# A two-layer decoder trunk: three plain gate/up pairs a layer instead of four, low parts of two operand preparations by ScalarE and an adding DMA, norm weights loaded by ScalarE's queue

## The chip, the cores and the metric

The kernel runs on one core of a Trainium2 chip. The metric is the device time of one execution in microseconds (us), the median of three runs. Engines are named as the profile names them: PE is TensorE's matmul, PEld its weight load, DVE is VectorE, ACT is ScalarE, POOL is GpSimd, SP is SyncE; SPq, POOLq and ACTq are the queues on which these engines issue transfers.

## What is computed

A decoder trunk of two layers works on 512 tokens of width 1024, in float32: a mixer (attention in layer 0, causal pooling in layer 1), then a gated feed-forward block (FFN), each on a normalized input and added back. The change lies in the FFN of both layers and in the first loads.

```
def swiglu_ffn(h, w_gate_up, w_down):
    gu = h @ w_gate_up
    gate, up = gu[..., :D_FF], gu[..., D_FF:]
    return (jax.nn.silu(gate) * up) @ w_down

for i in range(DEPTH):                      # DEPTH = 2, D_MODEL = 1024, SEQ = 512, D_FF = 2816
    x = x + mixer(rmsnorm(x, mixer_norm))   # attention, then pooling
    x = x + swiglu_ffn(rmsnorm(x, ffn_norm[i]), w_ffn_gate_up[i], w_ffn_down[i])
return rmsnorm(x, final_norm)
```

## The kernel before, in words

**Numbers.** Every float32 operand is split into a high part (a rounded copy, type fp32r) and a low part (what is left). A product is three matmuls: high by high, high by low, low by high. `split` (L90) makes the two parts: ACT copies the value into the high part (L91), DVE subtracts the high part from the value and writes the low part (L92). `split_neg` (L94 to L96) does the same for the negated value.

**FFN.** The 2816 hidden columns are 22 blocks of 128. For each block j there is one gate and one up product, together a pair. The first `NPLAIN` = 4 pairs of a layer are plain (`plain_pair`, L1047): two products of 8 steps over the 1024 input columns, so 2 x 8 x 3 = 48 matmuls of 128x512. The other 18 use a Strassen-like scheme with seven half-size products (`strassen_pair` L1128, which calls `chained` L515 and `mult` L453): 7 x 4 x 3 = 84 matmuls of 128x256. The scheme needs sums and differences of quarters of the normalized input, `T["11", k]`, `T["1", k]` and so on, k = 0 to 3. `chained` starts with the product called "11" (into the PSUM tile alpha), then "1" (into gamma), "2" (added onto alpha), "21", "3", "22" and last "4"; ACT copies alpha and gamma away in between (L531, L535, L539, L547).

**Preparing T.** `prepare(k)` (L1062) makes the operands of one k while the plain pairs run. It takes two temporary buffers, `Temp()`, h and t (called temp in the rows); there are two such buffers in all, so each prepare writes those of the one before it. `normed` (L570) fills h with two scaled quarters of X (L574, two instructions) and t with the differences (L578, L579, L581). Then three splits of 128x512 (one of h, two of t) and one `split_neg` of 128x256 write the high and low parts into the room called far. In the kernel before, `plain_pair(j)` calls `prepare(j)` between its gate and its up product.

**Order after the plain pairs.** The blocks run in four parts, `PARTS` (L43). Part 0 holds blocks 0 and 1: after the plain pairs, its down product follows (8 outputs x 2 steps x 3 = 48 matmuls of 128x512, each output added to X by DVE, L1173), and then the Strassen pairs. Engine orders come from a scheduler: each engine has one queue and waits on semaphores in it.

**Weights.** A plain weight tile is loaded by SP, copied to its high part by ACT (L145), negated into its low part by ACT (L146), and the weights themselves are added to that by a transfer on POOL's queue with `accum_op` add (L148); this is called lean. A Strassen pair (`class Pair`, L153) loads its blocks by SP (L169 to L171), makes the sums b by an adding transfer on POOL's queue (L172), and ACT and DVE split four tiles of them (L91, L92), with two additions on DVE (L188, L189). Raw weights go through a ring of four buffers, split weights through a ring of five; a load waits until the ring's oldest buffer has been read.

**Start.** POOL's queue loads the norm weights nrm (L891), four dummy matmuls (`WARM`) run on PE, and for each k SP loads X[k] and the weights `w_first[k]`, for k = 0 in two halves that ACT copies one by one (L914, L915). DVE scales X[0] by nrm (L387).

## Time and profile before

| what | value |
|---|---|
| median of three runs | 1189.78 us (1189.6 to 1190.49) |
| profiled execution, own time | 1190.54 us |
| its span (first to last instruction) | 1188.8 us |
| PE busy | 1179.8 us, 99% of the span |
| DVE busy | 966.0 us, 81% |
| ACT busy | 711.9 us, 60% |
| POOL busy | 171.6 us, 14% |
| mean granted TensorE clock | 0.998 of full |
| transfers on the adding queue (software_dynamic) | 61.38 MB, 31.2% of 16 engines' span |

Rows of the timeline give a start in us from the span's start, a duration in us, the engine, the line, and the operation with its tiles; several like instructions in a row are one row (x2), and square brackets tell how long the engine had been idle and what ended that. Durations of neighbours overlap a little, so what an engine spends on one instruction is read from start to start. DMA rows give the size and the median us from issue to landing.

### The profile page before, as it was taken

The page shows a single profiled execution, that of the slowest core. Times are in us where ns is not written, and L with a number is a line of the kernel's source. Part 1 is how long each engine was busy: PE and PEld are TensorE (multiplying, and loading weights), DVE is VectorE, ACT ScalarE, POOL GpSimd, SP SyncE. Part 2 cuts the span into 40 slices and gives each one's busy share as a digit, 9 for nine tenths or more (in the row PEclk, how much of TensorE's full clock was granted, in tenths as well). Part 3 has the DMA queues.
Part 4 walks back from the last instruction along what each step waited for, and adds up shares of the span by engine and source line. Part 5 has one row for each costly group of instructions (what it writes and reads, how often), then busy time and mean ns, then how long its engine had stood idle before and what let it go on. Part 6 is the DMA issues. An engine that isn't in the chain of part 4 may idle for free.

```text
span 1188.8 us, 24883 instructions
## 1 busy us (share of the span) xinstructions
PE 1179.8 (99%) x9932; PEld 1118.4 (94%) x9932; DVE 966.0 (81%) x1693; ACT 711.9 (60%) x1244; POOL 171.6 (14%) x171
## 2 busy tenths in 40 slices
PE   9999999999999999999999999999999999999997
PEld 7889999999999988889999999988888999999997
DVE  6978798889788855699988997656879998898875
ACT  6545564456455546647756775685675775676553
POOL 1111111111111002311111111122130111111100
PEclk9999999999999999999999999999999999999999
DMA  8446666665766548857777777798695777777732
GB/s 276 130 98 158 157 156 154 172 160 147 202 144 158 152 145 207 190 117 187 197 194 190 191 191 191 207 266 207 128 194 108 193 194 196 200 194 190 197 93 72
DMA packets 82036, 205.19 MB, mean 173 GB/s; under 512 B 7648, under 2 KB 13184, under 8 KB 81920
## 3 DMA queue, kind: packets, MB, share of 16 engines
q1 hardware_dynamic: 51232, 141.96, 36.2%
q0 software_dynamic: 30544, 61.38, 31.2%
q8 instruction: 78, 1.28, 0.4%
q14 instruction: 38, 0.31, 0.1%
q10 hardware_dynamic: 144, 0.26, 0.1%
HBM read 201.48 MB, written 2.10 MB: 171 GB/s over the span
## 4 chain that ended last, share of the span: by engine, by line
PE 97%; issue 1%; ACT 1%; DMA 1%; DVE 0%; SPq 0%; POOL 0%; DVEq 0%; POOLq 0%; ACTq 0%
PE ps L457 20%; PE ps L459 19%; PE ps L458 19%; PE ps L325 9%; PE ps L326 8%; PE ps L328 8%; PE ps L628 2%; PE ps L630 2%; PE ps L629 2%; PE ps L921 2%; PE ps L840 1%; PE ps L712 1%; PE ps L732 1%; PE ps L834 1%; DMA x<-xT 1%
## 5 line engine op out<-in xcount | busy, mean ns | idle before, releaser
L91 ACT ACTIVATE w<-raw 128x1024 fp32r<-128x1024 f32 x265 | 280.5, 1063 | 171.3 <-PE ps L459 69.4
L92 DVE TENSOR_TENSOR w<-raw,w 128x1024 fp32r<-128x1024 f32 x265 | 323.0, 1222 | 52.2 <-ACT w L91 47.9
L457 PE MATMUL ps<-far,w 128*128 128x256 f32 x896 | 247.1, 276 | 0.3 <-ACT first L531 0.3
L459 PE MATMUL ps<-far,w 128*128 128x256 f32 x896 | 247.0, 276 | 0.0
L458 PE MATMUL ps<-far,w 128*128 128x256 f32 x896 | 247.0, 276 | 0.0
L457 PE MATMUL ps<-near,w 128*128 128x256 f32 x640 | 180.7, 282 | 0.0
L458 PE MATMUL ps<-near,w 128*128 128x256 f32 x640 | 177.4, 277 | 0.0
L459 PE MATMUL ps<-near,w 128*128 128x256 f32 x640 | 177.4, 277 | 0.0
L457 PEld LDWEIGHTS ps<-far,w 128*128 128x128 f32 x896 | 168.3, 188 | 0.5 <-ACT first L531 0.5
L458 PEld LDWEIGHTS ps<-far,w 128*128 128x128 f32 x896 | 168.3, 188 | 0.1
L459 PEld LDWEIGHTS ps<-far,w 128*128 128x128 f32 x896 | 168.3, 188 | 0.0
L325 PE MATMUL ps<-near,w 128*128 128x512 f32 (+1 forms) x332 | 125.8, 380 | 0.0
L328 PE MATMUL ps<-near,w 128*128 128x512 f32 (+1 forms) x332 | 125.2, 377 | 0.0
L326 PE MATMUL ps<-near,w 128*128 128x512 f32 (+1 forms) x332 | 125.1, 377 | 0.0
L457 PEld LDWEIGHTS ps<-near,w 128*128 128x128 f32 x640 | 120.6, 188 | 0.4
L458 PEld LDWEIGHTS ps<-near,w 128*128 128x128 f32 x640 | 120.4, 188 | 0.0
L459 PEld LDWEIGHTS ps<-near,w 128*128 128x128 f32 x640 | 120.4, 188 | 0.0
L172 POOL DMA_DIRECT2D raw<-w_pair x36 | 43.5, 1209 | 292.9 <-DMA raw<-w_pair 84.7
L328 PEld LDWEIGHTS ps<-near,w 128*128 128x128 f32 x332 | 62.4, 188 | 11.5
L325 PEld LDWEIGHTS ps<-near,w 128*128 128x128 f32 x332 | 62.3, 188 | 11.5 <-ACT near L91 0.4
L326 PEld LDWEIGHTS ps<-near,w 128*128 128x128 f32 x332 | 62.5, 188 | 11.2 <-DVE near L92 0.2
L91 ACT ACTIVATE half<-rawhalf 128x512 fp32r<-128x512 f32 x81 | 51.0, 631 | 14.6 <-PE ps L459 12.5
(311 smaller groups left out, 2763.3 us busy)
## 6 DMA issues: line engine op xcount, KB each, us to landing
raw<-w_pair SPq DMA_DIRECT2D x80, 512.0 KB, 4.8
raw<-w_qkp SPq DMA_DIRECT2D x36, 512.0 KB, 4.2
raw<-w_pair POOLq DMA_DIRECT2D x36, 512.0 KB, 7.6
raw<-w_dblock SPq DMA_DIRECT2D x32, 512.0 KB, 4.8
raw<-w_v SPq DMA_DIRECT2D x18, 512.0 KB, 4.4
raw<-w_qkp POOLq DMA_DIRECT2D x18, 512.0 KB, 7.6
rawhalf<-w_pair SPq DMA_DIRECT2D x36, 256.0 KB, 5.2
raw<-w_dblock POOLq DMA_DIRECT2D x16, 512.0 KB, 7.6
```

Of the source, the lines that this page charges most:

```text
L91: nc.scalar.activation(hi, v, AF.Copy)
L92: nc.vector.tensor_tensor(lo, v, hi.bitcast(F32), op=OP.subtract)
L172: nc.gpsimd.dma_start(self.b.rearrange("p (a c) -> p a c", a=2), self.src[:, None, 3 * n:].to_broadcast([P, 2, n]), accum_op=OP.add)
L325: nc.tensor.matmul(self.p[:, cols], w[0][:, s], mh[:, cols], start=self.done == 0, stop=False)
L326: nc.tensor.matmul(self.p[:, cols], w[0][:, s], ml[:, cols], start=False, stop=False)
L328: nc.tensor.matmul(self.p[:, cols], w[1][:, s], mh[:, cols], start=False, stop=self.done == self.n)
L457: nc.tensor.matmul(dst, w.t[0][:, c], th, start=k == 0 and not on, stop=False, skip_group_check=on)
L458: nc.tensor.matmul(dst, w.t[0][:, c], tl, start=False, stop=False, skip_group_check=on)
L459: nc.tensor.matmul(dst, w.t[1][:, c], th, start=False, stop=k == n - 1, skip_group_check=on)
L628: nc.tensor.matmul(o, mh, wh, start=k == 0, stop=False)
L629: nc.tensor.matmul(o, mh, wl, start=False, stop=False)
L630: nc.tensor.matmul(o, ml, wh, start=False, stop=k == K2 - 1)
```

## The change

`NPLAIN` falls from 4 to 3, so that pair 3 of each layer becomes a Strassen pair; it then runs after the down product of part 0 instead of before it. The four prepares stand in three pairs: prepare(0) in pair 0, prepare(1) in pair 1, prepare(2) at the end of pair 1, prepare(3) in pair 2. In prepare(1) and prepare(2) the three 128x512 splits are made by `moved`: ACT writes the high part, ACT writes its negative into the low part, and a transfer on POOL's queue adds the value from the temporary buffer. Norm weights are loaded on ACT's queue, `w_first[0]` comes in one transfer with one ACT copy, and there are five dummy matmuls.

```
-NPLAIN = 4
-WARM = 4
+NPLAIN = 3
+WARM = 5
...
+    def moved(hi, lo, v):
+
+        nc.scalar.activation(hi, v, AF.Copy)
+        nc.scalar.activation(lo, hi.bitcast(F32), AF.Copy, scale=-1.0)
+        nc.gpsimd.dma_start(lo, v.bitcast(F32R), accum_op=OP.add)
...
-            nc.gpsimd.dma_start(nrm, norms)
+            nc.scalar.dma_start(nrm, norms)
...
                 nc.sync.dma_start(X[k], xT[:, k, :])
+                nc.sync.dma_start(raw[:, s], w_first[k])
                 if k:
-                    nc.sync.dma_start(raw[:, s], w_first[k])
                     scaled(0, k, *U[k])
                     nc.scalar.activation(hi[:, s], raw[:, s], AF.Copy)
                 else:
-                    for e in range(2):
-                        c = slice(e * NF * P // 2, (e + 1) * NF * P // 2)
-                        nc.sync.dma_start(raw[:, c], w_first[k][:, c])
-                        nc.scalar.activation(hi[:, c], raw[:, c], AF.Copy)
+                    nc.scalar.activation(hi[:, s], raw[:, s], AF.Copy)
                     scaled(0, k, *U[k], on_dve=True)
...
-                prepare(j)
+                prepare((0, 1, 3)[j])
...
                 nc.vector.tensor_mul(up, up, gt)
+                if j == 1:
+                    prepare(2)
...
+                parted = moved if k in (1, 2) else split
                 h, t = normed(op, k, row, Temp(), Temp(), True)
...
-                split(b[:, 0].rearrange("p (a c) -> p a c", a=2), b[:, 1].rearrange("p (a c) -> p a c", a=2), hq[:, :, 0])
+                parted(b[:, 0].rearrange("p (a c) -> p a c", a=2), b[:, 1].rearrange("p (a c) -> p a c", a=2), hq[:, :, 0])
...
-                    split(b[:, 0], b[:, 1], t.t[:, i * S:(i + 1) * S])
+                    parted(b[:, 0], b[:, 1], t.t[:, i * S:(i + 1) * S])
```

Lines of the changed kernel are six higher than before in the body (L574 becomes L580, L92 stays), and some late ones differ by three or six. The engine orders move at these places of layer 0's FFN; layer 1 has the same tiles with small exchanges.

**DVE around prepare(2).** Before, the rows from its first instruction (temp_6099 is its h, temp_6100 its t; names in square brackets are the semaphores waited for, DMASW ones belong to POOL's transfers, DMAHW ones to SP's):

```order
L574 SCALAR_TENSOR_TENSOR temp_6099<-x_5169,nrm_75,row_5959 128x512
L574 SCALAR_TENSOR_TENSOR temp_6099<-x_5173,nrm_75,row_5959 128x512
L578 TENSOR_TENSOR temp_6100<-temp_6099 128x2x256 [waits DVE_49]
L92 TENSOR_TENSOR far_5857<-temp_6099,far_5857 128x512 [waits Activation_49]
L579 TENSOR_TENSOR temp_6100<-temp_6100,temp_6099 128x256 [waits DVE_49]
L96 SCALAR_TENSOR_TENSOR far_5857<-temp_6099,far_5857 128x256 [waits Activation_49]
L581 SCALAR_TENSOR_TENSOR temp_6100<-temp_6100,temp_6099 128x256 [waits DVE_49]
L1056 TENSOR_TENSOR u_6060<-ps_6114,row_5959 128x512 [waits PE_49]
L92 TENSOR_TENSOR far_5857<-temp_6100,far_5857 128x512 [waits Activation_49]
```

The same place of the changed kernel, up to the first instruction of prepare(3) (temp_6060 and temp_6061 are prepare(2)'s, temp_6108 is prepare(3)'s h; w_6155 and raw_5906 belong to the weights of pair 3):

```order
L580 SCALAR_TENSOR_TENSOR temp_6060<-x_5168,nrm_75,row_5960 128x512 [waits DMASW3_49,DVE_49]
L580 SCALAR_TENSOR_TENSOR temp_6060<-x_5172,nrm_75,row_5960 128x512
L92 TENSOR_TENSOR near_82<-up_6008,near_82 128x512 [waits Activation_49]
L194 TENSOR_TENSOR raw_5906<-raw_5906,raw_5907 128x512 [waits DMAHW2_49,DMAHW3_49,DMAHW1_49,DMAHW4_49,DMAHW0_49,DMASW5_49]
L92 TENSOR_TENSOR w_6155<-raw_5907,w_6155 128x1024 [waits DMASW4_49,Activation_49]
L584 TENSOR_TENSOR temp_6061<-temp_6060 128x2x256 [waits DMASW5_49,DMASW4_49,DVE_49]
L102 SCALAR_TENSOR_TENSOR far_5853<-temp_6060,far_5853 128x256 [waits Activation_49]
L585 TENSOR_TENSOR temp_6061<-temp_6061,temp_6060 128x256 [waits DVE_49]
L1059 TENSOR_TENSOR u_6080<-ps_6123,row_5960 128x512 [waits PE_49]
L587 SCALAR_TENSOR_TENSOR temp_6061<-temp_6061,temp_6060 128x256 [waits DVE_49]
L1061 TENSOR_TENSOR u_6080<-u_6080,gt_6106 128x512 [waits DVE_49]
L580 SCALAR_TENSOR_TENSOR temp_6108<-x_5169,nrm_75,row_5960 128x512 [waits DMASW6_49,DVE_49]
```

The three subtractions L92 into far are gone, and the first writes to h and t wait for a transfer of POOL (DMASW), which the rows before did not.

**DVE in prepare(3).** Before, its t and the low parts made from it:

```order
L578 TENSOR_TENSOR temp_6174<-temp_6173 128x2x256 [waits DVE_49]
L92 TENSOR_TENSOR far_5857<-temp_6173,far_5857 128x512 [waits Activation_49]
L579 TENSOR_TENSOR temp_6174<-temp_6174,temp_6173 128x256 [waits DVE_49]
L96 SCALAR_TENSOR_TENSOR far_5857<-temp_6173,far_5857 128x256 [waits Activation_49]
L581 SCALAR_TENSOR_TENSOR temp_6174<-temp_6174,temp_6173 128x256 [waits DVE_49]
L92 TENSOR_TENSOR w_6224<-raw_5979,w_6224 128x1024 [waits DMASW0_49,Activation_49]
```

In the changed kernel (x_5168 and others are the sums of the down product, w_6200 belongs to pair 4; the last row makes the low part of T["1", 3] and T["2", 3]):

```order
L1179 TENSOR_TENSOR x_5167<-x_5167,ps_6163 128x512 [waits PE_49]
L584 TENSOR_TENSOR temp_6109<-temp_6108 128x2x256 [waits DMASW7_49,DMASW1_49]
L1179 TENSOR_TENSOR x_5168<-x_5168,ps_6185 128x512 [waits PE_49]
L585 TENSOR_TENSOR temp_6109<-temp_6109,temp_6108 128x256 [waits DVE_49]
L92 TENSOR_TENSOR w_6200<-raw_5978,w_6200 128x1024 [waits DMAHW7_49,DMASW0_49,Activation_49]
L587 SCALAR_TENSOR_TENSOR temp_6109<-temp_6109,temp_6108 128x256 [waits DVE_49]
L92 TENSOR_TENSOR far_5853<-temp_6109,far_5853 128x512 [waits Activation_49]
```

prepare(3) now stands among the additions of the down product, and its t waits for two transfers.

**POOL's queue.** Before, from the low parts of the plain weights to the second Strassen pair that still lacks its sums (a transfer waits for the semaphore that it counts up itself, so DMASW3 in a row is also that row's own):

```order
L148 DMA w_5915<-w_pair 128x1024 [waits DMASW0_49,PE_49,Activation_49]
L172 DMA raw_5979<-w_pair 128x2x512 [waits DMAHW3_49,DMAHW4_49,DMAHW2_49,DMAHW5_49,DMAHW1_49,DMAHW7_49,DMAHW0_49,DMASW1_49]
L148 DMA w_5973<-w_pair 128x512 [waits DMASW2_49,PE_49,Activation_49]
L148 DMA w_5973<-w_pair 128x512 [waits DMASW3_49]
L148 DMA w_6051<-w_down 128x4x256 [waits DMASW4_49,PE_49,Activation_49]
L172 DMA raw_6091<-w_pair 128x2x512 [waits DMAHW5_49,DMAHW3_49,DMAHW6_49,DMAHW1_49,DMASW5_49]
L148 DMA w_6086<-w_down 128x4x256 [waits DMASW6_49,PE_49,Activation_49]
L172 DMA raw_6239<-w_pair 128x2x512 [waits DMASW7_49,DMAHW3_49,DMASW1_49,DVE_49]
```

In the changed kernel:

```order
L154 DMA w_5916<-w_down 128x4x256 [waits DMASW0_49,PE_49,Activation_49]
L178 DMA raw_5979<-w_pair 128x2x512 [waits DMAHW2_49,DMAHW5_49,DMAHW1_49,DMAHW6_49,DMAHW0_49,DMASW1_49]
L154 DMA w_5974<-w_down 128x4x256 [waits DMASW2_49,PE_49,Activation_49]
L98 DMA far_5853<-temp_6011 128x2x256 [waits DMASW3_49,DVE_49,Activation_49]
L98 DMA far_5853<-temp_6012 128x512 [waits DMASW4_49,DVE_49,Activation_49]
L98 DMA far_5853<-temp_6012 128x512 [waits DMASW5_49,DVE_49,Activation_49]
L98 DMA far_5853<-temp_6060 128x2x256 [waits DMASW6_49,DVE_49,Activation_49]
L98 DMA far_5853<-temp_6061 128x512 [waits DMASW7_49,DVE_49,Activation_49]
L178 DMA raw_6171<-w_pair 128x2x512 [waits DMAHW0_49,DMASW0_49]
L98 DMA far_5853<-temp_6061 128x512 [waits DMASW1_49,DVE_49,Activation_49]
```

Six adding transfers of 256 KB from the temporary buffers are new, and the sums of pair 5 (raw_6171) stand between the last two of them.

## The prediction

> **What bounds the kernel now.** The page's busy shares come first, then its chain of waits.
>
> ```profile
> PE 1179.8 (99%) x9932; PEld 1118.4 (94%) x9932; DVE 966.0 (81%) x1693; ACT 711.9 (60%) x1244; POOL 171.6 (14%) x171
> PE 97%; issue 1%; ACT 1%; DMA 1%; DVE 0%; SPq 0%; POOL 0%; DVEq 0%; POOLq 0%; ACTq 0%
> ```
>
> PE is busy from end to end and holds 97% of the chain, so time is won by fewer matmul columns or lost by making PE wait. The second view is a window on the plain pairs of layer 0, from the first product's scaling to the last split of prepare(3) (columns: length, then busy us and instructions of PE, PEld, DVE, ACT, POOL).
>
> ```profile
> 486.94:516.33 29.39, 29.39 (x132) 24.32 (x131) 29.35 (x52) 21.21 (x32) 7.32 (x7) 1.00 0.92 182
> ```
>
> In this stage DVE is busy for 29.35 of 29.39 us, and the transfers for 0.92 of their engines' time. PE never waits, but only because T is finished ahead of need. How far ahead, the PE rows tell: first matmul of pair 1's up product, 120 matmuls later, and the first Strassen matmul.
>
> ```profile
> 488.87 0.39 PE L325 MATMUL ps<-near,w 128*128 128x512 f32 x1
> 516.07 0.39 PE L325 MATMUL ps<-near,w 128*128 128x512 f32 x1
> 526.95 0.28 PE L457 MATMUL ps<-far,w 128*128 128x256 f32 x1
> ```
>
> A 128x512 matmul costs 27.20/120 = 0.227 us. T was complete at 516.33, PE asked for it from 526.95: 10.6 us of slack.
>
> **Part 1, the pair that leaves.** A plain pair is 48 matmuls, 526.95 - 516.07 = 10.88 us. A Strassen pair is read from ACT's first copy in successive pairs:
>
> ```profile
> 538.07 0.38 ACT L531 COPY first<-ps 128x256 f32<-128x256 f32 x1 [0.20 <-PE ps L459]
> 557.16 0.37 ACT L531 COPY first<-ps 128x256 f32<-128x256 f32 x1 [0.26 <-PE ps L459]
> ```
>
> Two pairs take 19.09 us, one 9.55, of which 84 matmuls at 0.1133 (half of 0.227) are 9.52. So PE saves 1.36 us a layer, 2.7 in all. In exchange PE reaches the first Strassen matmul at 516.07 instead of 526.95: the slack is spent at once. Pair 3's weights change hands: four ACT passes and three additions on POOL's queue become four ACT copies, one addition, and 5.2 us of DVE (three tiles of 1.14 us, a half tile and two additions of 0.60, priced below); where these rows stand in DVE's queue they are counted in the walk.
>
> **Part 2, the moved low parts.** DVE and ACT intervals (start to start), then the prices of transfers on POOL's and SP's queues (from the page, the transfer table, and windows at 457.9, 492.4 and 488.4; the last row is what one issue costs POOL):
>
> ```profile
> 488.88 0.68 DVE L1056 TENSOR_TENSOR up<-ps,row 128x512 f32<-128x512 f32 x1
> 489.48 0.68 DVE L578 TENSOR_TENSOR temp<-temp 128x512 f32<-128x512 f32 x1
> 490.68 0.42 DVE L579 TENSOR_TENSOR temp<-temp 128x256 f32<-128x256 f32 x1
> 491.01 0.68 DVE L1050 TENSOR_TENSOR gt<-ps,row 128x512 f32<-128x512 f32 x1
> 494.77 1.41 DVE L574 SCALAR_TENSOR_TENSOR temp<-x,nrm,row 128x512 f32<-128x512 f32 x2
> 496.09 0.68 DVE L1056 TENSOR_TENSOR up<-ps,row 128x512 f32<-128x512 f32 x1
> 513.90 1.22 DVE L92 TENSOR_TENSOR w<-raw,w 128x1024 fp32r<-128x1024 f32 x1
> 515.04 1.29 DVE L92 TENSOR_TENSOR far<-temp,far 128x512 fp32r<-128x512 f32 x2
> 489.55 1.05 ACT L145 ACTIVATE w<-raw 128x1024 fp32r<-128x1024 f32 x1
> 490.50 0.61 ACT L91 ACTIVATE far<-temp 128x512 fp32r<-128x512 f32 x1
> 491.02 1.04 ACT L146 ACTIVATE w<-w 128x1024 fp32r<-128x1024 f32 x1
> 493.01 0.40 ACT L95 ACTIVATE far<-temp 128x256 fp32r<-128x256 f32 x1
> 493.32 0.62 ACT L91 ACTIVATE near<-up 128x512 fp32r<-128x512 f32 x1
> ```
>
> ```profile
> raw<-w_pair SPq DMA_DIRECT2D x80, 512.0 KB, 4.8
> raw<-w_pair POOLq DMA_DIRECT2D x36, 512.0 KB, 7.6
> w<-w_pair POOLq DMA_DIRECT2D x16, 256.0 KB, 6.5
> invcnt<-invcnt_in POOLq DMA_DIRECT2D x1, 8.0 KB, 4.3
> w<-w_pair POOLq DMA_DIRECT2D x2, 256.0 KB, 5.3
> w<-w_pair POOLq DMA_DIRECT2D x2, 256.0 KB, 9.7
> raw<-w_pair POOLq DMA_DIRECT2D x1, 512.0 KB, 10.5
> 519.53 1.20 POOL L172 DMA_DIRECT2D raw<-w_pair  x1 [10.10 <-DVE x L1173]
> ```
>
> DVE: 0.60 for 512 columns, 0.33 for 256, 1.32 for the two that fill h, 1.14 for a weight tile. ACT: 0.52, 0.31, 0.95. Six low parts leave DVE, 3.6 us a layer; ACT gains six passes, 3.1 us, in a window where it was busy for 21.21 of 29.39.
>
> What is added is a wait. A temporary buffer was free when DVE had subtracted from it; now it is free when the transfer that reads it has landed, and there are only two. A transfer from SBUF to SBUF that adds isn't in this trace. Its bounds: 4.3 us, the 8 KB load, from below, and 9.7, the 256 KB additions issued in this very stretch, from above. I take L = 6.5, the median of the 256 KB additions, the nearest in size and kind. Behind a waiting DVE instruction stand the sums of X (which free PSUM), the weights of pairs 3 and 4 and T itself, and PE waits for those.
>
> The walk, with the clock of before up to the last row that both orders share (494.77):
>
> - prepare(1)'s h is done at 496.18 (494.77 + 1.41). ACT's copy, the 256 copy and the negation end at 497.6; POOL issues, landing at 497.6 + 6.5 = 504.1. DVE meanwhile has 4.5 us of rows and is ready at 496.09 + 4.5 = 500.6. **First wait: 3.5 us.** prepare(2) starts at A = 504.1.
> - DVE's rows of prepare(2) take 6.45 us (1.32, five of 0.60, one of 1.14, three of 0.33), to 510.6. Its h lands at A + 1.3 + 1.4 + 6.5 = 513.3. **Second wait: 2.8.**
> - prepare(3)'s t waits for the last part of prepare(2)'s t. ACT negates that at A + 7.5 (5.9 of DVE's rows, its copy at 0.52 and the negation at 0.62, with a 256 copy between them), but POOL's queue has pair 5's sums ahead, whose SP load starts when DVE has read the raw buffer (A + 3.7) and takes 4.8, to A + 8.5. If the two adding transfers are served in turn (the 512 KB one quoted took 10.5 behind others, against 7.6), the first lands at A + 8.5 + 7.6 = 520.2 and the second 1.5 later (half of the 2.9 by which that row exceeds the median, for half the bytes; an estimate), at 521.7. If not in turn: A + 8.5 + 1.2 to issue + 6.5 = 520.3. I take 521.7. DVE is ready at 513.3 + 5.2 = 518.5. **Third wait: 3.2.**
> - From there 3.7 us of DVE rows (0.60, 0.60, 0.33, 1.14, 0.33, and 0.69 to the end of the split) give T["1", 3] at 525.4. PE has 516.07 + 22 x 0.1133 = 518.56 for the matmul that reads it. **PE loses 6.8 us.**
> - Then ACT: its copy of alpha stands behind the second high part (525.3) and a weight tile (0.95), and ends at 526.7; PE, ready at 525.6 for product "2", loses 1.1. Before "4", four products or 5.44 us later, at 532.1, ACT must copy alpha once more, behind a weight tile that waits for DVE's L189. DVE has 5.7 us of backlog after 525.3 (five sums of X, a split, a weight tile, an addition, a 256 split), then 0.33 and 0.60: 531.9; with 0.95 and 0.4 of ACT 533.3, a loss of 1.2. The next pair meets the same wait with less backlog; I put half, 0.6 (an estimate).
>
> The loss is 6.8 + 1.1 + 1.2 + 0.6 = 9.7, less 1.36: **8.3 us a layer**. Layer 1 has the same rows with the same spacing (7.74 us from the first to prepare(1), 7.83 above), so I double it: 16.7.
>
> ```profile
> 486.94 0.69 DVE L1050 TENSOR_TENSOR gt<-ps,row 128x512 f32<-128x512 f32 x1 [4.27 <-ACT row L426]
> 869.16 0.69 DVE L1050 TENSOR_TENSOR gt<-ps,row 128x512 f32<-128x512 f32 x1 [4.20 <-ACT row L426]
> 876.90 1.42 DVE L574 SCALAR_TENSOR_TENSOR temp<-x,nrm,row 128x512 f32<-128x512 f32 x2
> ```
>
> In general, with A = 497.6 + L, the first loss is 2L - 7.6 if transfers aren't served in turn: 1.0 for L = 4.3 and 11.8 for 9.7.
>
> The Trainium skill, page "DMA: Bandwidth & Descriptors", section "Anatomy of one DMA — SWDGE (gpsimd) path", prices such a transfer at 2.0 us plus its bytes over 436 GB/s, which for 256 KB is an estimate of 2.6 us. By it DVE would not wait at all, and the sum would be the -2.7 of part 1; no 256 KB row of this trace is under 5.3.
>
> **Part 3, the start.**
>
> ```profile
> 1.17 0.90 SPq L914 DMA_DIRECT2D raw<-w_first  x2
> 2.10 0.44 SPq L906 DMA_DIRECT2D x<-xT  x1
> 4.77 0.49 DVE L387 TENSOR_SCALAR early<-x,nrm 128x512 fp32r<-128x512 f32 x1 [3.58 <-DMA nrm<-norms]
> 5.40 3.83 PE L921 MATMUL ps<-early,w 128*128 128x512 f32 x12 [0.38 <-DVE early L387]
> 8.26 0.72 ACT L389 ACTIVATE early<-x,nrm 128x512 fp32r<-128x512 f32 x1 [2.42 <-DMA x<-xT]
> 10.07 6.23 PE L921 MATMUL ps<-early,w 128*128 128x512 f32 x26 [0.84 <-ACT w L910]
> ```
>
> Norm weights end the wait at 4.77, but the twelve matmuls that follow are through before 10.07, where PE waits for X[1], landed at 8.26. So earlier norm weights are worth nothing by themselves; a later first copy (one of 512 columns) and a fifth dummy are hidden by the same 0.84 us of idle PE and more. One issue less on SP moves X[1]'s issue from 2.10 to about 1.64. I take 0.3 of that 0.46, between nothing and all of it; and up to 0.5 lost if the cover is gone.
>
> **Sum.** 1190.54 + 16.7 - 0.3 = 1206.9, against the profiled execution, which stood 0.8 us above the median.
>
> **The rivals.** (a) *Short landings.* If the sources in SBUF land at the 4.3 us floor, the loss is 1.0 + 2.9 - 1.36 = 2.5 a layer, 1195.3. (b) *Long landings.* At 9.7: 11.8 + 2.9 - 1.36 = 13.3, 1216.9. The busy 0.92 of the transfers speaks for it, fewer weight transfers against it. (c) *The buffers are free in time.* Below L = 3.1 the first wait vanishes (500.6 - 497.6), and at 3.8 the first loss of PE does: then PE keeps its 1.36 and the time is 1190.54 - 2.7 - 0.3 = 1187.5, faster. The six DVE subtractions saved speak for it; all rows of POOL's queue, 4.3 and up, against. (d) *Saving eaten.* Buffers free in time, but ACT's copy before "4" still late by DVE's backlog, up to 1.2 a layer: 1190.
>
> **How the numbers follow.** Forecast (1199 to 1214): 0.74. (b) 0.08, (a) 0.08, (d) 0.05, (c) 0.05. The range 1195 to 1218 holds the forecast, (a) and the most of (b), and leaves (c), (d) and the longest landings out. Slower by over 0.2% (2.4 us, about what a measurement of this kernel can tell from no change): 0.90; within: 0.05; faster: 0.05.
>
> **What would show it.** Right: DVE rows L580 and L584 with idle time ended by a transfer into far, about 3.5, 2.8 and 3.2 us; PE idle 7 to 10 us at the first Strassen pair (L463 to L465) and nowhere else; landings of far<-temp near 6.5. Wrong: landings near 3, or PE without idle time there; a stretch from the first row scaling to the next layer's that isn't 8 to 9 us longer; a start that moves by over 0.5.

## The result, and the profile after

The changed kernel takes 1206.41 us (1205.25 to 1207.56), the kernel before 1190.13 us (1189.6 to 1191.18): a ratio of 1.0133, 95% interval 1.0121 to 1.0145. It is 16.3 us slower; 1206.9 was forecast. The profiled execution took 1205.25 us, and with the profiled execution of before (1190.54) the difference is 14.7 us.

Busy shares and chain of the changed kernel, from its page:

```profile
PE 1184.0 (98%) x10006; PEld 1124.8 (93%) x10006; DVE 967.5 (80%) x1697; ACT 718.2 (60%) x1263; POOL 180.1 (15%) x178
PE 92%; DMA 3%; DVE 2%; issue 2%; ACT 1%; POOL 0%; DVEq 0%; POOLq 0%; ACTq 0%; SPq 0%
```

PE held 97% of the chain and now holds 92%; transfers and DVE have 5% of it. To find the place, both kernels are cut at a row that both have once per normalization, POOL's power for `rcol`. First the kernel before: the rows that start layer 0's FFN, the mixer of layer 1, layer 1's FFN and the final norm.

```profile
482.76 1.39 POOL L413 TENSOR_TENSOR rcol<-var,nhalf 128x2 f32<-128x2 f32 x2 [7.51 <-DVE var L410]
809.06 1.38 POOL L413 TENSOR_TENSOR rcol<-var,nhalf 128x2 f32<-128x2 f32 x2 [8.13 <-DVE var L410]
865.05 1.38 POOL L413 TENSOR_TENSOR rcol<-var,nhalf 128x2 f32<-128x2 f32 x2 [13.67 <-DVE var L410]
1174.40 1.09 POOL L413 TENSOR_TENSOR rcol<-var,nhalf 128x1 f32<-128x1 f32 x2 [44.09 <-DVE var L410]
```

And the changed kernel:

```profile
481.27 1.38 POOL L419 TENSOR_TENSOR rcol<-var,nhalf 128x2 f32<-128x2 f32 x2 [2.19 <-DVE var L416]
815.40 1.37 POOL L419 TENSOR_TENSOR rcol<-var,nhalf 128x2 f32<-128x2 f32 x2 [8.11 <-DVE var L416]
871.39 1.37 POOL L419 TENSOR_TENSOR rcol<-var,nhalf 128x2 f32<-128x2 f32 x2 [10.05 <-DVE var L416]
1188.81 1.10 POOL L419 TENSOR_TENSOR rcol<-var,nhalf 128x1 f32<-128x1 f32 x2 [45.50 <-DVE var L416]
```

All before layer 0's FFN is 1.49 us shorter. The FFN stretch of layer 0 goes from 326.30 to 334.13 (+7.83), that of layer 1 from 309.35 to 317.42 (+8.07), and between them both have 55.99. So the loss is in the two FFNs, about 8 us each. These two stretches are the measure in every experiment below.

DVE's waits in layer 0 and, below the dots, in layer 1:

```profile
501.99 1.42 DVE L580 SCALAR_TENSOR_TENSOR temp<-x,nrm,row 128x512 f32<-128x512 f32 x2 [2.78 <-DMA far<-temp]
511.46 1.42 DVE L580 SCALAR_TENSOR_TENSOR temp<-x,nrm,row 128x512 f32<-128x512 f32 x2 [2.90 <-DMA far<-temp]
518.63 0.69 DVE L584 TENSOR_TENSOR temp<-temp 128x512 f32<-128x512 f32 x1 [1.89 <-DMA far<-temp]
...
891.27 1.42 DVE L580 SCALAR_TENSOR_TENSOR temp<-x,nrm,row 128x512 f32<-128x512 f32 x2 [2.06 <-DMA far<-temp]
898.71 1.42 DVE L580 SCALAR_TENSOR_TENSOR temp<-x,nrm,row 128x512 f32<-128x512 f32 x2 [0.88 <-DMA far<-temp]
910.38 0.69 DVE L584 TENSOR_TENSOR temp<-temp 128x512 f32<-128x512 f32 x1 [5.78 <-DMA far<-temp]
```

A temporary buffer is to be written again, and a transfer still reads it: 7.57 us in layer 0, 8.72 in layer 1. The chain of waits through layer 0's plain pairs (start, length, what; pieces under 0.05 us are left out) says in which order this reaches PE:

```profile
497.51 4.37 DMA far<-temp
501.99 0.14 DVE temp L580
...
504.01 0.60 DVE raw L194
504.61 1.15 DVE w L92
505.77 4.27 DMA raw<-w_pair
510.09 0.63 issue
510.76 0.56 POOL raw L178
511.31 0.13 issue
511.44 7.16 DMA far<-temp
518.63 0.69 DVE temp L584
```

Read it from the top. The first transfer lands, DVE goes on and reads a raw weight buffer; that lets SP load pair 5's weights into it; POOL adds pair 5's sums (L178); behind them on the same queue stands the last transfer of prepare(2), and it takes 7.16 us. PE's rows with idle time, layer 0 and below the dots layer 1:

```profile
516.80 0.38 PE L463 MATMUL ps<-far,w 128*128 128x256 f32 x1 [0.67 <-DVE x L1179]
520.97 0.38 PE L463 MATMUL ps<-far,w 128*128 128x256 f32 x1 [2.84 <-ACT far L91]
522.38 0.58 PE L464 MATMUL ps<-far,w 128*128 128x256 f32 x1 [1.03 <-DVE far L92]
523.65 0.58 PE L463 MATMUL ps<-far,w 128*128 128x256 f32 x1 [0.47 <-ACT first L537]
...
913.26 0.58 PE L463 MATMUL ps<-far,w 128*128 128x256 f32 x1 [6.05 <-ACT far L91]
914.13 0.58 PE L464 MATMUL ps<-far,w 128*128 128x256 f32 x1 [0.29 <-DVE far L92]
```

PE's pauses are 5.01 and 6.34 us, less than the 9.2 and 9.4 that are missing (7.83 and 8.07 and the 1.36 that the smaller column count saves). A part of the rest shows in a window of layer 0 cut at the pause (columns: length, busy us and count of PE, PEld, DVE, ACT, POOL, granted clock, DMA share, GB/s):

```profile
517.90:521.90 4.00, 0.61 (x3) 0.21 (x2) 3.27 (x6) 0.77 (x2) 0.00 (x0) 0.98 0.33 115
521.90:528.70 6.80, 5.85 (x26) 5.55 (x27) 6.09 (x10) 2.34 (x5) 0.00 (x0) 0.51 0.03 4
528.70:534.70 6.00, 6.00 (x54) 5.96 (x53) 4.78 (x8) 4.52 (x8) 1.21 (x1) 1.00 0.44 109
```

After the pause the granted clock is 0.51 for 6.8 us: 26 matmuls take 5.85 us, where 0.1133 each would be 2.95. In layer 1 it is 0.50 from 913.2 to 917.6. The Trainium skill, page "TensorE: Matmul & The Clock Gate", section "Part 1: The HAM clock gate (the "warmup" mystery)", says that an idle window of about 3.4 us halves the clock until PE has been busy for a window. The trace agrees as far as it shows it: 4.0 us with three matmuls in them came before. Whether those 2.9 us are a cost of their own is taken up under fill.

### The profile page after: what moved, and what is told of

It reads as the page before. It is cut to its first block, busy times and chain, and to the rows that moved or that the text cites. A ratio compares the mean times of both kernels' runs of the same rounds, so it can differ in the third digit from the quotient of the medians.

```text
span 1203.1 us, 25073 instructions
## 1 busy us (share of the span) xinstructions
PE 1184.0 (98%) x10006; PEld 1124.8 (93%) x10006; DVE 967.5 (80%) x1697; ACT 718.2 (60%) x1263; POOL 180.1 (15%) x178
## 4 chain that ended last, share of the span: by engine, by line
PE 92%; DMA 3%; DVE 2%; issue 2%; ACT 1%; POOL 0%; DVEq 0%; POOLq 0%; ACTq 0%; SPq 0%
PE ps L463 20%; PE ps L465 20%; PE ps L464 20%; PE ps L331 6%; PE ps L334 6%; PE ps L332 6%; PE ps L634 2%; PE ps L635 2%; PE ps L636 2%; DMA far<-temp 2%; PE ps L924 2%; PE ps L846 1%; PE ps L718 1%; DMA raw<-w_pair 1%; DVE temp L580 1%
## 5 line engine op out<-in xcount | busy, mean ns | idle before, releaser
L91 ACT ACTIVATE w<-raw 128x1024 fp32r<-128x1024 f32 x271 | 286.1, 1062 | 155.9 <-PE ps L465 64.7
L92 DVE TENSOR_TENSOR w<-raw,w 128x1024 fp32r<-128x1024 f32 x271 | 329.9, 1222 | 51.7 <-ACT w L91 48.0
L463 PE MATMUL ps<-far,w 128*128 128x256 f32 x944 | 262.6, 278 | 10.3 <-ACT far L91 8.9
L464 PE MATMUL ps<-far,w 128*128 128x256 f32 x944 | 261.9, 277 | 1.3 <-DVE far L92 1.3
L465 PE MATMUL ps<-far,w 128*128 128x256 f32 x944 | 261.5, 277 | 0.0
L463 PEld LDWEIGHTS ps<-far,w 128*128 128x128 f32 x944 | 179.0, 190 | 12.1 <-ACT far L91 9.3
L464 PEld LDWEIGHTS ps<-far,w 128*128 128x128 f32 x944 | 179.1, 190 | 1.9 <-DVE far L92 1.8
L465 PEld LDWEIGHTS ps<-far,w 128*128 128x128 f32 x944 | 179.1, 190 | 0.0
L463 PEld LDWEIGHTS ps<-near,w 128*128 128x128 f32 x640 | 120.5, 188 | 0.4
L465 PEld LDWEIGHTS ps<-near,w 128*128 128x128 f32 x640 | 120.3, 188 | 0.0
L464 PEld LDWEIGHTS ps<-near,w 128*128 128x128 f32 x640 | 120.3, 188 | 0.0
L331 PE MATMUL ps<-near,w 128*128 128x512 f32 (+1 forms) x300 | 113.2, 378 | 0.0
L334 PE MATMUL ps<-near,w 128*128 128x512 f32 (+1 forms) x300 | 112.5, 375 | 0.0
L332 PE MATMUL ps<-near,w 128*128 128x512 f32 (+1 forms) x300 | 112.5, 375 | 0.0
L178 POOL DMA_DIRECT2D raw<-w_pair x38 | 45.7, 1203 | 304.7 <-DMA raw<-w_pair 85.6
L332 PEld LDWEIGHTS ps<-near,w 128*128 128x128 f32 x300 | 56.5, 188 | 10.1 <-DVE near L92 0.2
L331 PEld LDWEIGHTS ps<-near,w 128*128 128x128 f32 x300 | 56.3, 188 | 10.3 <-ACT near L91 0.4
L334 PEld LDWEIGHTS ps<-near,w 128*128 128x128 f32 x300 | 56.3, 188 | 10.2
```

The costliest lines, as they stand in the source:

```text
L91: nc.scalar.activation(hi, v, AF.Copy)
L92: nc.vector.tensor_tensor(lo, v, hi.bitcast(F32), op=OP.subtract)
L178: nc.gpsimd.dma_start(self.b.rearrange("p (a c) -> p a c", a=2), self.src[:, None, 3 * n:].to_broadcast([P, 2, n]), accum_op=OP.add)
L331: nc.tensor.matmul(self.p[:, cols], w[0][:, s], mh[:, cols], start=self.done == 0, stop=False)
L332: nc.tensor.matmul(self.p[:, cols], w[0][:, s], ml[:, cols], start=False, stop=False)
L334: nc.tensor.matmul(self.p[:, cols], w[1][:, s], mh[:, cols], start=False, stop=self.done == self.n)
```

## The experiments

The theory, called BUFFERS: two temporary buffers, held until adding transfers land, make DVE wait, and T comes late. Its rivals are that three plain pairs leave DVE too little time in any form (SLACK), that the transfers are late on POOL's queue whatever the buffers (QUEUE, also called CONTENTION or CONGESTION), and that the half clock makes a good part of the loss (CLOCK). START and QUEUE ORDER are theories of single experiments. All of them are in one table; the ratios are to the kernel before on the same chip, and the last two columns are the stretches from `rcol` to `rcol`, from one profile each. The engine orders are made anew for each kernel, so a variant can differ from its parent in more places than its edit.

| kernel | time, us | ratio (95%) | layer 0 | layer 1 |
|---|---|---|---|---|
| before | 1190.13 | 1 | 326.30 | 309.35 |
| changed | 1206.41 | 1.0133 (1.0121 to 1.0145) | 334.13 | 317.42 |
| start_only | 1189.23 | 0.9988 (0.9980 to 0.9997) | 326.31 | 309.35 |
| nrm_only | 1189.50 | one run | 326.31 | 309.35 |
| load_only | 1190.40 | one run | 326.26 | 309.35 |
| all_split | 1193.89 | 1.0029 (1.0021 to 1.0038) | 327.81 | 311.38 |
| fill | 1209.16 | 1.0164 (1.0148 to 1.0181) | 335.25 | 319.98 |
| moved_only | 1215.03 | 1.0208 (1.0192 to 1.0223) | 337.31 | 322.42 |
| last_split | 1198.95 | 1.0069 (1.0056 to 1.0081) | 333.23 | 311.44 |
| more_buffers | 1192.55 | 1.0017 (1.0008 to 1.0026) | 331.76 | 308.41 |
| four_both | 1187.97 | 0.9980 (0.9971 to 0.9989) | 326.20 | 308.45 |
| four_last | 1188.11 | 0.9981 (0.9972 to 0.9989) | 325.46 | 308.54 |
| four_split | 1194.20 | 1.0035 (1.0023 to 1.0048) | 327.89 | 314.11 |
| moved_four | 1207.34 | 1.0142 (1.0125 to 1.0159) | 334.54 | 317.26 |

**all_split**: the low parts back on DVE, all else as changed.

```
-                parted = moved if k in (1, 2) else split
+                parted = split
```

> The changed kernel with its six moved low parts subtracted by DVE again; three plain pairs, the order of prepare and the start stay. Theory BUFFERS (the loss comes from two temporary buffers held by transfers): DVE's waits on far<-temp (7.6 us in layer 0, 8.7 in layer 1) go, six subtractions of 0.6 (3.6) come back, T[1,3] is ready about 4 us earlier, PE loses 0.6 to 1.6 us a layer against the 1.36 saved, the start keeps its 1.5: 1186 to 1191. Rival SLACK (three plain pairs leave DVE too little time in any form, the transfers only show it): the stretches stay 8 us longer, 1203 or more.

Measured 1193.89, above the range that BUFFERS gave and far below SLACK's. DVE's waits on transfers are gone, PE has no pause for T, and 12.5 us of the loss with them. But three plain pairs are still not worth their 1.36 a layer: the stretches are 1.51 and 2.03 longer than before. The window of the plain pairs says why:

```profile
485.80:515.10 29.30, 29.30 (x130) 23.95 (x129) 29.24 (x52) 17.01 (x28) 3.51 (x3) 1.00 0.52 96
```

DVE is busy for 29.24 of 29.30 us. It was as busy before (29.35 of 29.39), but the fourth pair's 10.9 us of respite behind it are gone, and its backlog reaches PE as small stalls: in layer 0 two of 0.3 us for ACT's copies of alpha, and in layer 1 one of 0.4 for such a copy and one of 1.85 us, where a product waits for DVE to read PSUM. These listed stalls are not all of the 2.9 and 3.4 us by which the layers miss the saving; the rest isn't itemized. So SLACK is real: 4.7 us over start_only, about a quarter of the 17.2 that the changed kernel is over it.

**moved_only**: the kernel before with `moved` and `parted` alone; four plain pairs, `prepare(j)`, start of before.

> The kernel before (four plain pairs, its start, its order of prepare) with the moved low parts alone, for the second and third operand. Theory BUFFERS: DVE's waits on far<-temp appear, 3 to 9 us a layer, but the 10.6 us of slack that the fourth plain pair gives cover them, and DVE saves 3.6: 1190 within 1.5, PE without idle time at the first Strassen pair. Rival CONTENTION (the adding transfers hold up weight loads and X's sums, whatever the slack): 1195 or more, with PE waiting elsewhere.

Measured 1215.03, and the expectation of BUFFERS falls: with the slack of a fourth pair the moved low parts cost more, not less, and the rival's "1195 or more, with PE waiting elsewhere" is what came. DVE's waits are 8.64, 3.42 and 1.24 us in layer 0. A DVE that waits also holds up the plain pairs: PE waited 7.7 us, over both layers, for DVE to read products out of PSUM (L1062). Slack of T does not cover a wait of the engine that serves everything else, too. And the transfers themselves come later, median 6.4 us to landing in this stretch against 4.4 in the changed kernel; see moved_four.

**last_split**: one of the six moved parts, the last of prepare(2), by DVE.

```
-                    parted(b[:, 0], b[:, 1], t.t[:, i * S:(i + 1) * S])
+                    (split if k == 2 and i else parted)(b[:, 0], b[:, 1], t.t[:, i * S:(i + 1) * S])
```

> The changed kernel with one of the six moved low parts, the last half of the third operand's t, subtracted by DVE again. In the changed kernel the transfer of that part is issued right behind pair 5's sums and lands after 7.2 us (layer 0), and the fourth operand's t waits for it, 1.89 and 5.78 us. Theory QUEUE ORDER (that one transfer sets the end): the third wait goes to under 0.5 us, DVE gives 0.6 for the subtraction, T[1,3] comes 1.3 us earlier in layer 0 and 5.2 in layer 1: 1198 to 1201. Rival: the transfer ahead of it on the queue or the first two waits set the end anyway: 1204 or more.

Measured 1198.95, inside the range of QUEUE ORDER. The third wait is gone in both layers; layer 1 wins 5.98 us, layer 0 only 0.90 of the 1.3 expected. There the first two waits remain (3.38 and 2.95 us), and PE then waits 5.20 us for sums of X that now stand behind T's rows on DVE. So the transfer behind pair 5's sums was most of layer 1's loss and a small part of layer 0's.

**more_buffers**: four places for temporary buffers, taken in turn, at the expense of two places for operands.

```
-NEAR = 11
-OPEN = 2
+NEAR = 10
+OPEN = 4
...
-SLOTS = 15
+SLOTS = 14
...
-        if dtype == F32 or open:
+        if dtype == F32:
+            turns[0] += 1
+            order = loose[turns[0] % OPEN:] + loose[:turns[0] % OPEN]
+        elif open:
             order = loose
```

> The changed kernel with four places for temporary buffers taken in turn (two places fewer for operands); in layer 0 an operand holds one of them, so there are three, in layer 1 four. Theory BUFFERS: in layer 1 DVE's waits on far<-temp (2.06, 0.88, 5.78 us in the changed kernel) go to nothing or near it, PE no longer pauses for T[1,3] (6.05 us), and the stretch from rcol to rcol, 317.42 us there and 309.35 before, comes to 308 to 310; in layer 0 the waits fall by more than half and the stretch of 334.13 by 4 or more; in all 1188 to 1196. Rival CONGESTION (the transfers themselves, behind one another and behind pair sums in POOL's queue, give T late whatever the buffers): T[1,3] stays late in layer 1 and the time over 1202.

Measured 1192.55, with a contrast inside one run. In layer 1, where all four places are free, DVE never waits for a transfer, PE never pauses, and the stretch is 308.41: 9.0 us less than in the changed kernel and 0.94 less than before. In layer 0, where an operand holds one place, two waits remain, 5.06 us of 7.57, where less than half was expected, and the stretch falls by 2.4 to 331.76, less than the 4 expected:

```profile
502.82 0.69 DVE L588 TENSOR_TENSOR temp<-temp 128x512 f32<-128x512 f32 x1 [2.76 <-DMA far<-temp]
513.37 1.42 DVE L584 SCALAR_TENSOR_TENSOR temp<-x,nrm,row 128x512 f32<-128x512 f32 x2 [2.30 <-DMA far<-temp]
```

**four_both**: more_buffers, and the fourth place freed in layer 0 by another placement of two heads of the attention output.

```
-                    held["o", h], b = slot("oh", open=h == 3)
+                    held["o", h], b = slot("oh", open=h in (3, 6, 7))
```

> As more_buffers, with two heads of the attention output placed so that all four places are free for temporary buffers in layer 0 too. Theory BUFFERS: layer 0 now does what layer 1 did in more_buffers (rcol to rcol 308.41 against 309.35 before): no DVE wait on far<-temp, no pause of PE for T[1,3], a stretch of 325.4 to 326.5 instead of 331.76, the start's 1.2 kept: 1186 to 1188, faster than before. Rival: layer 0 has another bound (its sums of X and weight splits stand behind T on DVE), and its stretch stays over 329: 1190 or more.

Measured 1187.97: faster than the kernel before, ratio 0.9980 (0.9971 to 0.9989). Of the gain the start gives 1.2 us (start_only), and the two stretches 0.10 and 0.90. All that is left of DVE's waits in both layers is

```profile
502.91 1.42 DVE L584 SCALAR_TENSOR_TENSOR temp<-x,nrm,row 128x512 f32<-128x512 f32 x2 [0.23 <-DMA far<-temp]
505.54 0.69 DVE L588 TENSOR_TENSOR temp<-temp 128x512 f32<-128x512 f32 x1 [0.61 <-DMA far<-temp]
```

and the same transfers do it at the same median time to landing (4.2 us over all twelve, 4.2 in the changed kernel). BUFFERS holds for the changed kernel: the twelve transfers are harmless, and what cost 8 us a layer was that their sources were wanted back.

**four_last** and **four_split**: four_both with one part, and with all six, by DVE again.

> As four_both, with the last half of the third operand's t subtracted by DVE, so that no transfer of T stands behind pair 5's sums. With four buffers nobody waits for that transfer before PE does, so theory BUFFERS expects no gain, at most 0.6 us of DVE more a layer: equal to four_both within 1.5. If the queue's order still cost something (T[4,2] late for PE), this one is the faster by 1 or more.

> As four_both, with all six low parts subtracted by DVE (no transfer reads a temporary buffer). Theory: buffers cost nothing where no transfer holds them, so this repeats all_split (1193.9, ratio 1.0029): DVE busy without a pause through the plain pairs and 3.6 us a layer more to do, small stalls of PE for weights and sums in the first Strassen pairs. It should be slower than four_both by 4 to 7 us; that is what moving the low parts is worth when its wait is gone. If it equals four_both, the other placement of operands made the gain and the transfers did nothing.

four_last, 1188.11, equals four_both: once the buffers are free, the place on the queue costs nothing that is seen. four_split, 1194.20, repeats all_split (1193.89), so the new placement of operands wins nothing by itself; its profiled execution took 1195.30, and there layer 1 is 2.7 us longer than in all_split, for a reason that isn't settled. The moved low parts are worth 6.2 us when nobody waits for them (1194.20 - 1187.97). The saving that the change was made of is there.

**moved_four**: moved_only with the buffers of four_both.

> moved_only (four plain pairs, moved low parts, the start of before: 1215.0) with the four free buffers of four_both. In moved_only POOL's queue issued the second operand's first transfer at 501.4 us, 3.7 after its source was ready, behind weight additions of the plain pairs, and it landed 7.6 later; DVE waited 8.64, 3.42 and 1.24 us for buffers. Theory BUFFERS: with four places only the fourth operand's h waits for that first transfer, some 5 us, which the 10.6 us of slack cover: 1189 to 1192. Rival QUEUE (with the fourth plain pair's additions on POOL's queue the transfers are late whatever the buffers, and a DVE that waits holds up the plain pairs' products as well): 1196 or more, DVE still waiting 8 us or more a layer.

Measured 1207.34: four buffers win 7.7 us on moved_only, but QUEUE holds for the version with four plain pairs. POOL's queue in layer 0:

```profile
498.19 1.31 POOL L154 DMA_DIRECT2D w<-w_down  x1 [4.48 <-DVE far L102]
499.71 1.20 POOL L98 DMA_DIRECT2D far<-temp  x1 [0.21 <-ACT far L97]
505.72 1.22 POOL L178 DMA_DIRECT2D raw<-w_pair  x1 [4.81 <-issue]
506.45 2.32 POOL L98 DMA_DIRECT2D far<-temp  x2
```

The first transfer, issued at 499.71 behind a 512 KB weight addition, is waited for until 508.24, 8.5 us later, and the next ones are issued only at 506.45. Ahead of them in the queue stand the sums L178, which lack weights that SP loads from 495.09 to 502.80 by the run's chain of waits; from there to 505.70, for 2.9 of the 4.81 us, POOL waits for nothing that the profile shows. DVE waits 10.7 and 10.5 us for transfers in the two layers, as QUEUE said. PE's longest pauses, 4.0 and 4.4 us, are for ACT's copy of alpha ahead of product "3" (L549), which in layer 0 stands behind a split that waits for DVE. Over all twelve transfers the median is 6.7 us, against 4.2. Against the kernels with three plain pairs there are the fourth pair's lean weight additions on that queue, the sums of a pair stand between the first and the second transfer, and prepare(2) stands in another place; the run doesn't tell these apart. Why POOL stands still stays open too.

**fill**: extra matmuls in PE's pause, so that the clock is kept.

```
+            if fill and name == "1" and k == n - 1:
+                for i in range(fill.pop()):
+                    c = slice(half * w.n + i % k * P, half * w.n + (i % k + 1) * P)
+                    nc.tensor.matmul(dst, w.t[0][:, c], T[name, i % k][0], start=False, stop=False, skip_group_check=on)
```

> The changed kernel with 33 (layer 0) and 54 (layer 1) extra 128x256 matmuls put where PE waits for T[1,3]; they repeat products of the parts 0 to 2 of that operand and so add products to the result that the reference doesn't have. They take 3.7 and 6.1 us at 0.1133 and fit into the waits of 3.9 and 6.3. Theory CLOCK (in the changed kernel the granted clock is 0.50 from 521.9 to 528.7, and the stretches are 7.83 and 8.07 us longer although PE waits only 5.0 and 6.3 and saves 1.36): with PE kept busy the clock stays at 1.00 and the time falls by 4.2 + 3.1 = 7 us, to 1199.5. Rival: the half clock is no cost of its own (PE would wait for T's consumers anyway), or it comes without a pause: 1206.4 unchanged.

Measured 1209.16, where CLOCK said 1199.5. But the run is not the test that was meant; nor is its result the kernel's, since the extra products are added to it. In layer 0 the granted clock stayed at 1.00, and PE ran into another wait in the same pair:

```profile
529.50 0.42 ACT L91 ACTIVATE near<-t 128x256 fp32r<-128x256 f32 x1 [5.09 <-DVE t L1108]
529.83 0.35 ACT L551 COPY first<-ps 128x256 f32<-128x256 f32 x1
530.23 0.39 PE L469 MATMUL ps<-far,w 128*128 128x256 f32 x1 [3.00 <-ACT first L551]
```

That is ACT's copy of alpha ahead of product "3". In fill's order it stands behind a split (near) that waits for DVE; in the changed kernel the same copy (L545, at 526.61) stands ahead of that split and followed PE at once. So this wait is fill's own. In layer 1 the same copy costs 1.52 us, and there the clock was not kept: it was 0.50 from 918 to 921. So fill does not settle CLOCK. The changed kernel's own rows put a bound on it:

```profile
529.06 0.42 DVE L549 TENSOR_TENSOR gt<-ps,first 128x256 f32<-128x256 f32 x1 [1.07 <-PE ps L465]
530.18 1.06 ACT L91 ACTIVATE w<-raw 128x1024 fp32r<-128x1024 f32 x1 [3.20 <-DVE raw L195]
531.15 0.35 ACT L553 COPY sums<-ps 128x256 f32<-128x256 f32 x1
531.55 0.38 PE L463 MATMUL ps<-far,half 128*128 128x256 f32 x1
...
919.36 0.42 DVE L549 TENSOR_TENSOR gt<-ps,first 128x256 f32<-128x256 f32 x1 [0.22 <-PE ps L465]
```

The PE row is the first matmul of product "4". It needs ACT's copy L553, the copy stands behind a weight tile that waits for DVE's L195, and L195 stands behind L549 in DVE's queue. There DVE waited for PE only 1.07 us in layer 0 and 0.22 in layer 1. A PE at full clock could have started "4" earlier by no more than that, so in this order of the queues the half clock costs at most 1.1 and 0.2 us of its own (an estimate), where CLOCK said 4.2 and 3.1. The rest of its time lies behind DVE's backlog. As for fill's extra 2.7 us, DVE waited 1.3 us more for transfers (17.6 us against 16.3); how much of the other 1.4 is the changed order isn't settled.

**start_only**, and its two halves **nrm_only** (norm weights by ACT's queue) and **load_only** (one first load and one copy).

> The kernel before with part 3 of the change alone (norm weights by ScalarE's queue, one first weight load, one copy, five dummies). Theory START: in the changed kernel layer 0's rcol stands at 481.27 against 482.76 us, 1.49 earlier, and all of that is part 3: the time falls by 1.5 us, to 1188.6. Rival, the prediction's own part 3: 0.3, 1189.8; the other 1.2 us would then be noise between two profiles.

> The kernel before with the norm weights by ScalarE's queue alone. Start as a whole gained 1.0 us at rcol (481.74 against 482.76), and X[1]'s first reader stands at 5.54 us against 8.26. If the norm weights do it: X[1] read by 6 us and rcol of layer 0 near 481.8. If the single first weight load does it: X[1] still read near 8.3 and rcol near 482.7.

> The kernel before with the single first weight load and single copy alone (norm weights by POOL's queue, four dummies). If one issue less on SP is what counts: X[1] read about 0.5 to 2.7 us earlier than 8.26 and rcol of layer 0 near 481.8 to 482.3. If the norm weights' queue is what counts: X[1] read near 8.3 and rcol near 482.7.

start_only took 1189.23, ratio 0.9988 (0.9980 to 0.9997): 1.2 us, between the 1.5 of START and the 0.3 of its rival, and nearer to START. Of the halves there is one run each. The windows from 5 to 12 us, of before, nrm_only, load_only and start_only:

```profile
5.00:12.00 7.00, 5.79 (x21) 4.42 (x21) 4.59 (x8) 4.16 (x8) 0.00 (x0) 1.00 0.98 345
```

```profile
5.00:12.00 7.00, 6.42 (x25) 4.45 (x25) 4.73 (x8) 4.79 (x9) 0.00 (x0) 1.00 0.99 342
```

```profile
5.00:12.00 7.00, 6.37 (x21) 5.11 (x21) 6.94 (x12) 6.24 (x12) 0.00 (x0) 1.00 1.01 358
```

```profile
5.00:12.00 7.00, 7.00 (x28) 5.45 (x27) 6.19 (x10) 6.13 (x11) 0.00 (x0) 1.00 1.00 356
```

Count PE's matmuls in these 7 us: 21, 25, 21, 28. Layer 0's `rcol` follows: 482.76 before, 481.60 with the norm weights alone, 482.68 with the load alone, 481.74 with both. The load alone brings X[1]'s first reader from 8.26 to 5.65 us, but PE then waits for the norm weights (read at 5.02 there, at 3.98 in nrm_only), and its matmuls come more slowly, for a reason that isn't settled. The norm weights alone start PE earlier, and X[1] is read at 7.01, though SP issued it at the same time as before (2.11 us); why it lands sooner isn't settled either. Kernels with the old start have their `rcol` between 482.26 and 482.76 (moved_four and moved_only too), those with the new one between 480.79 and 481.74, so single profiles agree to about half a microsecond on either side, and the 1.16 us of nrm_only is known no better than that.

## Why the prediction came out right, and where its steps didn't

The mechanism of the loss was forecast and is shown; that the sum came within 2 us is in part luck, since terms that were off cancelled.

**PE is bound, and DVE has no room in the plain pairs.** Right: all_split shows what 29.24 of 29.30 us mean.

**Part 1, 1.36 us a layer.** Right as a sum of columns, but taken for itself it isn't to be had. The 10.6 us of slack of the fourth pair also let DVE work off its weights and sums; all_split is 1.51 and 2.03 longer than before instead of 1.36 shorter. Only when six subtractions left DVE without a wait (four_both) did layer 1 gain 0.90, and layer 0 0.10. That is the case of rival (d), the saving eaten by DVE's backlog although the buffers are free in time: it eats 0.46 us in layer 1 and 1.26 in layer 0 there, for the "up to 1.2" that it was given, and PE does wait 0.7 us in layer 0 for ACT's copy before "4" (L557). With the subtractions back on DVE (all_split) it is 2.9 and 3.4.

**The walk of part 2.** The mechanism is the one that was forecast, with the waits in the forecast order and, in layer 0, at nearly the forecast size: 2.78, 2.90 and 1.89 us for 3.5, 2.8 and 3.2. Two terms were off and cancelled. The first transfer landed after 4.37 us, not 6.5, but POOL issued it 1.4 us later than the walk had it (at 497.51, which is 499.0 on the clock of before, against 497.6). ACT's negation ended on time, at 496.16; the row of the transfer has POOL idle for 1.68 us before it and puts that down to DVE's L585, which the walk did not have there. The path through pair 5's load and sums is in the chain as it was told; that load took 4.27 us for 4.8, and from POOL's turn for the sums (510.71) to the landing of the transfer behind them it took 7.9 us, where the two assumptions of the walk came to 7.7 and 9.1. L is thus not one number: in the changed kernel the transfers take 4.4 at the start of the stretch and 7.2 behind a 512 KB addition. 6.5 was the median of weight additions on a queue that also served a fourth plain pair; moved_only and moved_four, which have that queue, show medians of 6.7 over their twelve transfers. The fourth pair is not all of the difference, though, for the same weight additions still take 6.2 in the changed kernel. Two of the rows behind the bounds of L were misread. The transfer table of before has

```profile
nrm<-norms POOLq DMA_DIRECT2D x1, 24.0 KB, 3.5
rawhalf<-w_v SPq DMA_DIRECT2D x8, 256.0 KB, 3.3
```

so POOL's queue does have a row under 4.3, and "no 256 KB row of this trace is under 5.3" holds for POOL's queue alone.

**PE's loss.** 9.7 us a layer was forecast, 9.2 and 9.4 measured, in other parts. PE lost 3.9 and 6.3 us at T["1", 3] for 6.8. Of the three waits for ACT's copies (1.1, 1.2, 0.6) the first is there with 0.47 in layer 0. The second doesn't show as a pause: ACT's copy before "4" came as late as it was told, behind the weight tile that waits for DVE (it ended at 531.50, which is 533.0 on the clock of before, for 533.3), but PE, at half clock, came to "4" no sooner, at 531.55. The half clock, which the prediction had not thought of, takes the place of that wait. The third doesn't show either. Layer 1 was doubled from layer 0, and the sums agree, but not the waits: 2.06, 0.88 and 5.78.

**Part 3.** This term failed: -0.3 forecast, 1.2 to 1.5 measured. The step that failed is that "earlier norm weights are worth nothing by themselves", because PE waits for X[1] at 10.07. By themselves they moved `rcol` by 1.16 in one run; the earlier issue of X[1], on which the 0.3 rested, moved it by 0.08 in another. The row with the gap at 10.07 was read as if X[1]'s landing were fixed: in nrm_only the first matmuls came earlier and X[1] did as well, and PE went on at 9.16.

**The sum.** In the profiles the FFNs give 15.9 for the 16.7 forecast, the start 1.5 for 0.3; that would be 1205.0, and the profiled execution took 1205.25, 1.6 under the forecast, which was made for it. The median is 1.2 higher. Rival (a), short landings, had half the truth: 4.4 us was right, but the loss did not fall with it, since the transfer behind pair 5's sums took over. Rival (c), buffers free in time, is four_both: its 1187.5 was within 0.5 us of what was measured once there were four, but by luck, for the two stretches gave 1.0 us instead of 2.7 and the start 1.2 instead of 0.3.

## What to carry to other kernels

When work moves from an engine to a transfer, the source buffer lives until the transfer lands: count the buffers for the new lifetime first, since two buffers made this change 16 us slower than before and four made it 2 us faster, 1.2 us of that by the start. An engine that waits for such a buffer is late for everything else in its queue, so slack of the one result does not cover it. And take a transfer's time from the queue as it will be after the change, with what stands ahead of it, not from a median of other traffic.

## What the runs showed of the hardware

- A 256 KB transfer from SBUF to SBUF that adds took 3.3 us (four_last) to 9.1 us (fill) from issue to landing, with medians of 3.9 to 4.5 in the kernels with three plain pairs and 6.7 in the two with four. The longest one of the changed kernel, 8.5 us in layer 1, was issued 0.7 us behind a 512 KB addition on the same queue. The price of 2.6 us, worked out from the Trainium skill's page "DMA: Bandwidth & Descriptors" in the prediction, was not seen in any run.
- After 4.0 us with three matmuls PE's granted clock was 0.51 for 6.8 us. The longest single pause doesn't tell: after a pause of 3.00 us in layer 0 of fill the clock stayed at 1.00, while in layer 1 it was 0.50 from 918 to 921, although no pause there was over 0.76 us; PE had been busy for 1.50 us of the 3.10 from 914.4 to 917.5. In the changed kernel most of the slow time lay behind DVE, which was late anyway.
- POOL stands still now and then while it waits for nothing that the profile shows: for 2.9 to 3.5 us after the load that it lacked had landed in moved_only and moved_four, and for 4.08 us (the row at 890.65) already in the kernel before. What holds it is open.
